# Splitting the first branch's operands during a retention instead of during the rope

## The chip, the cores and the metric

The kernel runs on one core of a Trainium2 chip. The metric is the time of one execution on the device, in microseconds (us). TensorE, the matrix engine, is PE in the profile and its weight loads are PEld; VectorE is DVE, ScalarE is ACT, GpSimd is POOL, and SP is the engine that issues nearly all DMAs.

## What is computed

One block of a hybrid network on 528 tokens (16 meta tokens and 512 of the sequence) with 1024 channels. Cut to what matters here:

```python
z = rms_norm(h) @ w_in
u_rnn, u_gate, q, k, v, g_ret, ga, gb = split(z)
o_a = rg_lru(causal_dwconv(u_rnn)) * gelu(u_gate)
q, k = rotary(q), rotary(k)
o = retention(q, k, v)
o_b = head_rms(o) * silu(g_ret)
mixed = sigmoid(ga) * (o_a @ w_branch_rnn) + sigmoid(gb) * (o_b @ w_branch_ret)
h = h + mixed @ w_out
out = rms_norm(h + conv_ffn(rms_norm(h)))
```

The first branch is `o_a` and its product with `w_branch_rnn`, ten blocks of 128 channels. The retention has four heads.

## The kernel before, in words

Activations stand with channels on the 128 partitions and tokens along the row. TensorE works on fp16 operands: each fp32 operand is split into a high and a low fp16 part, and a product is three matmuls, high by high, high by low and low by high. `split` (L91) makes the two parts: the high one on ACT (L92), a scaled copy, and the low one on DVE (L93), the scaled source minus the high part. Weights come by DMA into two buffers `raw`, are split into ten buffers `wt`, and `tick` moves this on by a step between products.

The stages follow each other in the program: the recurrent branch; its gate; the rope, in which `rotary` (L726) projects q and k of each head in turn (L401) and turns them on DVE (L742 to L744); then scores, values and retention for the heads in the order written at L1014 to L1029; then the branches' products, the output product and the feed-forward part. Up to the rope the order on PE, ACT and DVE is the order of the code. From the rope on, a scheduler sets the order of each engine's instructions when the program is built. Each engine then works in that order.

During the rope of heads 0 and 1, `branch_a` (L713) is called for the ten blocks of the first branch, two or three at a time. It multiplies a block's gate by its recurrent state on DVE (L715; the gate's buffer holds the product) and splits the product into a new buffer `oa`. The parts are first read by `branch` in the stage of gates and branch products, at 426.4 us.

`scores(h)` (L771) makes three groups of products in accumulators `ps`, weighs them on DVE with the decay (`sf`, L794) and splits them (`sc`). `values(h)` makes `v`. `retention_out(h)` (L921) takes four tiles in turn; for each it runs 24 matmuls (L937) and yields after ACT has copied the result to `or` (L941) and squared it (L943) and DVE has added the square to `ssum` (L945). Before the first retention the accumulators are laid out anew, two large ones (`acc`) and four single banks: the new ones lie where the old ones did and wait for these to be read. `gated(0)` follows: `fast_products` (L844) runs gate products in the banks `pa`, `pb` and `pe`, with `kept` and `last` copied out by ACT (L857) and sums on DVE (L874, L878, L885), and `head_norm` (L948) multiplies `ssum` by a matrix of ones on TensorE (L952), takes the root on ACT (L954) and its reciprocal on DVE (L956). Retention of the next head is run between these products.

Of the kernel before, what the change touches and what calls it, by code (L numbers as in the profile page):

```python
# [9 lines left out]
F16 = mybir.dt.float16  # L10
# [4 lines left out]
P = 128  # L15
# [11 lines left out]
TQ = T - T0  # L27
# [9 lines left out]
S_OA = 1.0  # L37
# [14 lines left out]
def hybrid_block_kernel(ctx, tc, x, meta, norm_mix_g, w_in, conv_w, conv_b, rg_a_w, rg_a_b,  # L52
# [12 lines left out]
    def psum_layout(**pools):  # L65

        if "scope" in psum:
            psum["scope"].close()
        psum["scope"] = ExitStack()
        for nm, bufs in pools.items():  # L70
            psum[nm] = psum["scope"].enter_context(tc.tile_pool(
                name="psum_" + nm, bufs=bufs, space=bass.MemoryType.PSUM, reuse_waits="tile"))

    def acc(name):
        return psum["acc"].tile([P, 2, 512], F32, name=name, tag="acc")
# [9 lines left out]
    def piece(shape, dtype, name):  # L85
        return pieces.tile(shape, dtype, name=name, tag="s")

    def wtile(name):
        return work.tile([P, T], F32, name=name, tag="w")

    def split(hi, lo, src, s):  # L91
        a = nc.scalar.activation(hi, src, AF.Copy, scale=s)  # L92
        b = nc.vector.scalar_tensor_tensor(lo, src, s, hi, op0=ALU.mult, op1=ALU.subtract)  # L93
        return a.ins, b.ins
# [193 lines left out]
    def get(u):  # L288
        current[0] = max(current[0], u)
        while len(loaded) <= u:  # L290
            queue(unit_load())
        while done[0] < len(steps) and steps[done[0]][0] <= u:
            emit_step()
        return wviews[u]

    def tick(n=1):

        for _ in range(n):
            if done[0] == len(steps):
                if len(loaded) == len(units):  # L300
                    return
                queue(unit_load())
            u = steps[done[0]][0]
            if sum(unit_tiles(i) for i in range(current[0], u + 1)) > ahead[0]:
                return
            emit_step()
# [401 lines left out]
                for i in range(m0, m0 + 5):  # L708
                    f(i)

    oa = {}

    def branch_a(n):  # L713
        g = gate_g.pop(n)[:, :TQ]
        nc.vector.tensor_mul(g, g, half_x.pop(n)[:, T0:])  # L715
        oa[n] = piece([P, 2, TQ], F16, "oa")
        split(oa[n][:, 0], oa[n][:, 1], g, S_OA)

    order.close()

# [28 lines left out]
    for h in range(HEADS):  # L749
        t = [[piece([P, 2, T], F16, f"qk{h}{i}{m}") for m in range(2)] for i in range(2)]  # L750
        qk.append(t)
        rotary(u_q[h], t[0], HQ, TQ, T0, S_QK / (SW * S_XN))
        if h < 2:
            for n in range(5 * h, 5 * h + 2):
                branch_a(n)
        rotary(u_k[h], t[1], HT, T, 0, S_QK / 16.0 / (SW * S_XN))
        if h < 2:
            for n in range(5 * h + 2, 5 * h + 5):
                branch_a(n)
# [11 lines left out]
    def scores(h):  # L771
        st = sc[h] = [piece([P, 2, n], F16, f"sc{h}") for n in (SOFF[1], SOFF[2] - SOFF[1], SC - SOFF[2])]
        q, k = qk[h]
        krep = work.tile([P, 2, 2, P], F16, name="krep", tag="w")
        for m in range(2):
            nc.vector.tensor_copy(krep[:, m].rearrange("p a (r t) -> p a r t", t=NM),
                                  k[m][:, :, None, T - NM:T].broadcast_to([P, 2, P // NM, NM]))

        def group(pieces):
            ps = acc("ps")  # L780
            for bank, b, c0, n in pieces:
                j0 = JB[b][0]
                i = 0
                for m in range(2):
                    for kk, qq in ((0, 0), (0, 1), (1, 0)):
                        kv = k[m][:, kk, j0:j0 + P] if b < 4 else krep[:, m, kk]
                        nc.tensor.matmul(ps[:, bank, :n], kv,
                                         q[m][:, qq, I0[b] - T0 + c0:I0[b] - T0 + c0 + n],
                                         start=i == 0, stop=i == 5)
                        i += 1  # L790
            for bank, b, c0, n in pieces:
                dc = I0[b] - JB[b][0] + c0
                f = wtile("sf")
                nc.vector.scalar_tensor_tensor(f[:, :n], ps[:, bank, :n], S_S / (S_QK * S_QK),  # L794
                                               dec[h][:, dc:dc + n] if b < 4 else dec_meta[:, h, :n],
                                               op0=ALU.mult, op1=ALU.mult)
                sb = st[SCP[b][0]]
                o = SOFF[b] + c0 - SCP[b][1]
                split(sb[:, 0, o:o + n], sb[:, 1, o:o + n], f[:, :n], 1.0)

        group([(0, 0, 0, 257), (1, 0, 257, 257)])
        group([(0, 1, 0, T - I0[1]), (1, 2, 0, T - I0[2])])
        group([(0, 3, 0, T - I0[3]), (1, 4, 0, T - I0[4])])
# [10 lines left out]
    def make_forms(g):  # L814

        if not x_form_t:
            for i in range(2):
                x_form_t[i] = xslot([P, 4, 4, 257], F16, f"xs{i}")
        ks = slice(2 * g, 2 * g + 2)
        t = {}  # L820
        for i in range(2):
            for j in range(2):
                v = t[i, j] = wtile("xt")[:, :TQ].rearrange("p (k c) -> p k c", k=2)
                k0, (c0, n) = 4 * j + 2 * g, HQ[i]
                nc.vector.tensor_tensor(v, xh[:, k0:k0 + 2, c0:c0 + n], xl[:, k0:k0 + 2, c0:c0 + n], op=ALU.add)
        a11, a12, a21, a22 = t[0, 0], t[0, 1], t[1, 0], t[1, 1]
        nc.vector.tensor_tensor(a22, a22, a21, op=ALU.subtract)
        nc.vector.tensor_tensor(a21, a11, a21, op=ALU.subtract)
        nc.vector.scalar_tensor_tensor(a11, a22, -1.0, a11, op0=ALU.mult, op1=ALU.subtract)
        nc.vector.scalar_tensor_tensor(a12, a11, -1.0, a12, op0=ALU.mult, op1=ALU.subtract)  # L830
        for i, v in enumerate((a12, a22, a11, a21)):
            xs = x_form_t[i // 2]
            split(xs[:, 2 * (i % 2), ks], xs[:, 2 * (i % 2) + 1, ks], v, 1.0)
# [58 lines left out]
    def values(h):  # L892
        vt = []
        wa, wb = get(u_v[h][0]), get(u_v[h][1])
        for b, (j0, nb) in enumerate(JB):
            if b % 2 == 0:
                ps = acc("ps")
            pb = ps[:, b % 2]
            vt.append(piece([P, 2, 512], F16, f"v{h}"))
            i = 0  # L900
            if b == 4:
                for r, wr in enumerate((wa, wb)):
                    for a in range(2):
                        for g in range(4):
                            m = 2 * NM if a == 0 else NM
                            xs = xlast[:, 4 * r + g].rearrange("p a t -> p (a t)")
                            nc.tensor.matmul(pb[32 * g:32 * g + m], xs[:, :m], wr(a, g, 0, 512),
                                             start=r == 0 and a == 0, stop=r == 1 and a == 1,
                                             tile_position=(0, 32 * g))
                split(vt[b][:, 0], vt[b][:, 1], pb, S_V / (SW * S_XN))  # L910
                continue
            for k in range(KD):
                w = wa if k < 4 else wb
                for ax, aw in SPLIT:
                    nc.tensor.matmul(pb, xf(ax, k, XF + j0, nb), w(aw, k % 4, 0, 512), start=i == 0, stop=i == 23)  # L915
                    i += 1
            split(vt[b][:, 0], vt[b][:, 1], pb, S_V / (SW * S_XN))
            tick()
        vv[h] = vt
# [72 lines left out]
    def gated(h):  # L992

        other = retention_out(h + 1)
        for i in range(2):
            a = gate_unit(h, i)
            next(a)
            if i == 0:
                head_norm(h)
            for _ in range(2):  # L1000
                next(a)
                tick()
            next(other)
            scale_head(h, i)
            for _ in range(2):
                next(a)
                tick()
            next(other)
            for _ in a:
                pass  # L1010
        for _ in other:
            pass
# [5 lines left out]
    scores(2)  # L1018
    make_forms(1)
    values(1)  # L1020
    scores(3)
    psum_layout(acc=2, bank=4)
    ahead[0] = 9
    for _ in retention_out(0):
        pass
    gated(0)
    values(2)
    gated(1)
# [601 lines left out]
```

## Time and profile before

| | us |
|---|---|
| median of 3 runs | 1068.04 |
| lowest and highest run | 1067.8, 1068.93 |
| the profiled execution, its own time | 1068.13 |
| its span in the profile | 1066.4 |
| TensorE busy, share of the span | 98% |
| DVE, ACT, POOL | 81%, 55%, 1% |
| mean granted TensorE clock | 0.999 |

The span is what the profiler saw of the execution; the time of a run holds some 1.7 us around it. A busy TensorE is not one at its peak, since matmuls overlap. An engine that is busy all through a stretch does not bind it if TensorE is busy all through it too.

### The profile page before, as it was taken

What the parts mean: (1) busy time and instruction counts of PE and PEld (TensorE: products, weight loads), DVE (VectorE), ACT (ScalarE), POOL (GpSimd) and SP (SyncE); (2) the same over time, 40 slices, a digit from 0 to 9 for tenths busy, and PEclk for the clock granted to TensorE, in tenths of its full rate; (3) what the DMA queues carried; (4) which work ended last, traced back from release to release, by engine and by line L of the source; (5) the groups of instructions that cost most, each with busy time, mean ns of one, the idle gap of its engine ahead of it and who ended that gap; (6) DMA issues with size and microseconds to landing.
All of it is one profiled execution on the core that took longest, in us unless ns stands there. A gap on an engine that the chain in (4) does not pass through costs nothing.

```text
span 1066.4 us, 21008 instructions
## 1 busy us (share of the span) xinstructions
PE 1049.7 (98%) x8995; PEld 851.7 (80%) x8995; DVE 860.2 (81%) x1289; ACT 589.1 (55%) x927; POOL 6.9 (1%) x20
## 2 busy tenths in 40 slices
PE   9999999999999999999999999999999999999997
PEld 6888888865684848888888886588888888888884
DVE  6885799998786969887787886479989897988975
ACT  8568954434564747566454453366566465454442
POOL 2000000000000000000000000000000000000000
PEclk9999999999999999999999999999999999999999
DMA  8331243431211322333333365032432324214322
GB/s 255 102 133 45 80 139 119 160 120 40 78 43 47 113 65 65 115 94 109 115 110 115 105 221 179 1 119 80 159 111 88 120 81 136 64 60 137 102 80 80
DMA packets 108989, 111.49 MB, mean 105 GB/s; under 512 B 5610, under 2 KB 100560, under 8 KB 108896
## 3 DMA queue, kind: packets, MB, share of 16 engines
q1 hardware_dynamic: 108448, 109.74, 32.0%
q8 instruction: 70, 1.15, 0.4%
q10 hardware_dynamic: 160, 0.27, 0.1%
q0 software_dynamic: 288, 0.14, 0.1%
q14 instruction: 23, 0.19, 0.1%
HBM read 108.04 MB, written 2.10 MB: 103 GB/s over the span
## 4 chain that ended last, share of the span: by engine, by line
PE 78%; DVE 14%; ACT 6%; issue 2%; ACTq 0%; DVEq 0%
PE ps L401 31%; PE P L1466 9%; PE pa L852 9%; PE pm L401 4%; PE ps L915 4%; PE ps L1189 4%; PE pe L852 4%; DVE wt L93 3%; PE ps L414 3%; PE pb L852 2%; PE pa L1353 2%; ACT wt L92 2%; PE ps L937 1%; DVE rnn L648 1%; PE pe L1353 1%
## 5 line engine op out<-in xcount | busy, mean ns | idle before, releaser
L401 PEld LDWEIGHTS <-wt 128*128 128x128 f16 x3840 | 373.2, 97 | 58.2 <-DVE t L742 1.4
L93 DVE SCALAR_TENSOR_TENSOR wt<-raw,wt 128x1024 f16<-128x1024 f32 (+2 forms) x278 | 303.9, 1105 | 64.9 <-ACT wt L92 63.6
L92 ACT ACTIVATE wt<-raw 128x1024 f16<-128x1024 f32 (+2 forms) x278 | 263.4, 962 | 151.3 <-PE P L1466 25.3
L852 PEld LDWEIGHTS <-wt 128*128 128x128 f16 x2016 | 195.0, 97 | 34.7 <-issue 7.4
L401 PE MATMUL ps<-x2h,wt 128*128 128x258 f16 x1184 | 181.2, 273 | 0.0
L401 PE MATMUL ps<-xh,wt 128*128 128x257 f16 (+2 forms) x1056 | 163.8, 275 | 1.1 <-DVE t L742 1.1
L401 PE MATMUL ps<-x2l,wt 128*128 128x258 f16 x592 | 113.2, 272 | 0.0
L401 PE MATMUL ps<-xl,wt 128*128 128x257 f16 (+2 forms) x528 | 102.2, 275 | 0.0
L1466 PE MATMUL P<-wt,act 128*128 128x256 f16 x792 | 88.3, 273 | 0.0
L1466 PEld LDWEIGHTS <-act 128*128 128x128 f16 x792 | 77.5, 98 | 9.0
L915 PE MATMUL ps<-wt,xh 128*128 128x512 f16 x256 | 76.1, 379 | 2.3 <-DVE v L93 2.3
L1331 DVE SCALAR_TENSOR_TENSOR cv<-ps,vt,cv 128x512 f32<-128x512 f32 x80 | 59.7, 747 | 22.8 <-ACT cv L1329 21.9
L852 PE MATMUL pa<-xs,wt 128*128 128x257 f16 x576 | 71.6, 273 | 3.4 <-ACT kept L857 3.1
L401 PE MATMUL pm<-oa,wt 128*128 128x257 f16 x480 | 55.4, 274 | 0.0
L1329 ACT ACTIVATE cv<-ps,vt,vt 128x512 f32<-128x512 f32 x40 | 31.0, 774 | 34.5 <-PE ps L401 33.8
L915 PEld LDWEIGHTS <-xh 128*128 128x128 f16 x256 | 24.8, 98 | 31.4 <-issue 3.4
L915 PE MATMUL ps<-wt,xl 128*128 128x512 f16 x128 | 48.3, 379 | 0.0
L256 DVE TENSOR_TENSOR raw<-raw 128x1024 f32<-128x1024 f32 x39 | 47.6, 1220 | 0.7
L852 PE MATMUL pa<-ob,wt 128*128 128x257 f16 x384 | 45.7, 274 | 0.6 <-ACT last L857 0.5
L1189 PE MATMUL ps<-wt,mx 128*128 128x512 f16 x192 | 44.3, 378 | 0.0
L1353 PEld LDWEIGHTS <-wt 128*128 128x128 f16 x336 | 32.6, 97 | 4.4
L1189 PEld LDWEIGHTS <-mx 128*128 128x128 f16 x192 | 17.7, 98 | 18.4
(290 smaller groups left out, 1417.1 us busy)
## 6 DMA issues: line engine op xcount, KB each, us to landing
raw<-in_w_in SPq DMA_DIRECT2D x40, 1024.0 KB, 4.9
raw<-in_w_up SPq DMA_DIRECT2D x24, 1024.0 KB, 5.2
raw<-in_w_down SPq DMA_DIRECT2D x48, 256.0 KB, 3.5
raw<-in_w_branch_ret SPq DMA_DIRECT2D x16, 512.0 KB, 4.5
raw<-in_w_branch_rnn SPq DMA_DIRECT2D x8, 640.0 KB, 4.6
raw<-in_w_out SPq DMA_DIRECT2D x4, 1024.0 KB, 4.9
xin<-in_x SPq DMA_DIRECT2D x4, 512.0 KB, 5.5
raw<-in_w_in SPq DMA_DIRECT2D x4, 512.0 KB, 8.1
```

The lines of the kernel that those rows point to most:

```text
L92: a = nc.scalar.activation(hi, src, AF.Copy, scale=s)
L93: b = nc.vector.scalar_tensor_tensor(lo, src, s, hi, op0=ALU.mult, op1=ALU.subtract)
L256: nc.vector.tensor_tensor(pair, pair, rv[:, :, right].rearrange("p (h k) c -> p h k c", h=2), op=ALU.add)
L401: nc.tensor.matmul(ps[:, hf, :n], w(aw, k, col, P), src(ax, k, c0, n), start=k == 0 and (aw, ax) == (0, 0), stop=k == nk - 1 and aw == 1)
L414: mm = nc.tensor.matmul(ps[:, hf, :n], w(aw, k, col, P), src(ax, k, c0, n), start=k == 0 and (aw, ax) == (0, 0), stop=k == KD - 1 and aw == 1)
L852: nc.tensor.matmul(ps[:, :257], ws[k // 4](wf, aw, k % 4), src(xf_, ax, k), start=first and k == 0 and (aw, ax) == (0, 0), stop=k == last_ ...
L915: nc.tensor.matmul(pb, xf(ax, k, XF + j0, nb), w(aw, k % 4, 0, 512), start=i == 0, stop=i == 23)
L1189: nc.tensor.matmul(ps[:, n], mx[k][:, a, c0:c0 + P], wo[k // 2](aw, k % 2, n * 512, 512), start=k == 0 and (a, aw) == (0, 0), stop=k == ks ...
L1329: nc.scalar.activation(vv_, src[:, :, 2:258], AF.Identity, scale=vt2[:, 96 + ch:97 + ch], bias=bias)
L1331: nc.vector.scalar_tensor_tensor(vv_, src[:, :, j:j + 256], vt2[:, 48 * j + ch:48 * j + ch + 1], vv_, op0=ALU.mult, op1=ALU.add)
L1353: nc.tensor.matmul(ps[:, :258], w(wf, aw, k), x2_form(xf_, ax, k), start=first and k == 0 and (aw, ax) == (0, 0), stop=k == 3 and aw == 1, ...
L1466: nc.tensor.matmul(pd[:, 256 * tt:256 * tt + 256], t[:, ax, c0 + tt * P:c0 + tt * P + P], w(wf, aw, i), start=q % 6 == 0 and tt == 0 and i ...
```

## The change

`branch_a` keeps the product and no longer splits it. A new `split_a` splits the next two products that are not split yet. It is called once after `values(1)` and, in place of `pass`, after each of the four tiles of the first retention, for all ten.

```diff
-    oa = {}
+    oa, products_a = {}, []
 
     def branch_a(n):
         g = gate_g.pop(n)[:, :TQ]
         nc.vector.tensor_mul(g, g, half_x.pop(n)[:, T0:])
-        oa[n] = piece([P, 2, TQ], F16, "oa")
-        split(oa[n][:, 0], oa[n][:, 1], g, S_OA)
+        products_a.append(g)
+
+    def split_a(m=2):
+        for _ in range(m):
+            n = len(oa)
+            oa[n] = piece([P, 2, TQ], F16, "oa")
+            split(oa[n][:, 0], oa[n][:, 1], products_a[n], S_OA)
...
     values(1)
+    split_a()
     scores(3)
     psum_layout(acc=2, bank=4)
     ahead[0] = 9
     for _ in retention_out(0):
-        pass
+        split_a()
     gated(0)
```

Lines behind `branch_a` stand five further down in the changed kernel, those behind the call after `values(1)` six. Three places of the order show it. The first is DVE in the rope of head 0, from the last split of its q to the splits of its k; `oa<-rnn` are the splits, `rnn<-rnn` the multiplications, `t` the rope's products. Before:

```order
L93 SCALAR_TENSOR_TENSOR oa<-rnn,oa 128x514 x2
L742 TENSOR_TENSOR t_2092<-ps,rope_1850 128x528
L715 TENSOR_TENSOR rnn<-rnn 128x514
L93 SCALAR_TENSOR_TENSOR wt<-raw,wt 128x1024 x2
L715 TENSOR_TENSOR rnn<-rnn 128x514
L743 TENSOR_TENSOR t_2093<-ps,rope_1851 128x528
L742 TENSOR_TENSOR t_2097<-ps,rope_1850 128x528
```

and changed:

```order
L747 TENSOR_TENSOR t_2086<-ps,rope_1850 128x528
L715 TENSOR_TENSOR rnn<-rnn 128x514
L93 SCALAR_TENSOR_TENSOR wt<-raw,wt 128x1024 x2
L715 TENSOR_TENSOR rnn<-rnn 128x514 x3
L748 TENSOR_TENSOR t_2087<-ps,rope_1851 128x528
L747 TENSOR_TENSOR t_2091<-ps,rope_1850 128x528
```

Two splits have gone and two multiplications, which stood further back, have come ahead of the last two products. The second place is DVE at the end of `values(1)`, where the scores of head 3 begin. Before:

```order
L93 SCALAR_TENSOR_TENSOR v_3372<-ps,v_3372 128x512
L93 SCALAR_TENSOR_TENSOR v_3403<-ps,v_3403 128x512
L794 SCALAR_TENSOR_TENSOR sf<-ps,dec_2873 128x257 x2
L794 SCALAR_TENSOR_TENSOR sf<-ps,dec_2873 128x400
L93 SCALAR_TENSOR_TENSOR sc_3422<-sf,sc_3422 128x257 x2
```

and changed:

```order
L93 SCALAR_TENSOR_TENSOR v_3342<-ps,v_3342 128x512
L93 SCALAR_TENSOR_TENSOR v_3373<-ps,v_3373 128x512
L93 SCALAR_TENSOR_TENSOR oa<-rnn,oa 128x514 x2
L799 SCALAR_TENSOR_TENSOR sf<-ps,dec_2843 128x257 x2
L799 SCALAR_TENSOR_TENSOR sf<-ps,dec_2843 128x400
L93 SCALAR_TENSOR_TENSOR sc_3398<-sf,sc_3398 128x257 x2
```

Two splits stand ahead of the `sf` products. The third place is ACT in the first retention, from the first tile's copy to the first `kept`. Before:

```order
L941 ACTIVATE or_3498<-ps 128x514
L943 ACTIVATE ssum<-ps 128x514
L941 ACTIVATE or_3499<-ps 128x514
L943 ACTIVATE sq<-ps 128x514
L941 ACTIVATE or_3500<-ps 128x514
L943 ACTIVATE sq<-ps 128x514
L941 ACTIVATE or_3501<-ps 128x514
L943 ACTIVATE sq<-ps 128x514
L857 ACTIVATE kept<-pa 128x257
```

and changed:

```order
L946 ACTIVATE or_3474<-ps 128x514
L948 ACTIVATE ssum<-ps 128x514
L92 ACTIVATE oa<-rnn 128x514 x2
L946 ACTIVATE or_3475<-ps 128x514
L948 ACTIVATE sq<-ps 128x514
L92 ACTIVATE oa<-rnn 128x514 x2
L946 ACTIVATE or_3476<-ps 128x514
L948 ACTIVATE sq<-ps 128x514
L92 ACTIVATE oa<-rnn 128x514 x2
L946 ACTIVATE or_3477<-ps 128x514
L948 ACTIVATE sq<-ps 128x514
L92 ACTIVATE oa<-rnn 128x514 x2
```

A pair of splits stands behind each tile's square, the last one ahead of `kept`. On TensorE one matmul of the product `pe` stands ahead of the ones matmuls of `head_norm` that stood behind them; nothing else moves there.

## Rows read from the trace of the kernel before

**Rows 1.** The page, part 1: busy time, share of the span, instructions.

```profile
PE 1049.7 (98%) x8995; PEld 851.7 (80%) x8995; DVE 860.2 (81%) x1289; ACT 589.1 (55%) x927; POOL 6.9 (1%) x20
```

**Rows 2.** Windows: length, busy time per engine (instructions), granted clock, DMA share, GB/s.

```profile
161.70:226.70 65.00, 65.00 (x578) 56.13 (x579) 63.41 (x88) 27.62 (x39) 0.00 (x0) 1.00 0.47 156
226.70:285.70 59.00, 58.35 (x369) 30.55 (x367) 50.91 (x101) 26.93 (x49) 0.00 (x0) 1.00 0.11 39
380.00:385.00 5.00, 3.55 (x17) 1.55 (x16) 3.49 (x6) 0.93 (x2) 0.00 (x0) 1.00 0.00 0
```

**Rows 3.** The chain of waits, 130 to 330 us: start, length, what.

```profile
161.70 65.04 PE ps L401 x576
...
293.43 0.60 ACT or L941
...
295.39 1.11 PE ps L952 x4
```

**Rows 4.** Order of time in the rope: start, length, instruction, [idle before <-releaser].

```profile
161.70 0.40 PE L401 MATMUL ps<-xh,wt 128*128 128x257 f16 x2 [1.12 <-DVE t L742]
...
164.02 1.14 ACT L92 ACTIVATE oa<-rnn 128x514 f16<-128x514 f32 x2
...
165.10 1.29 DVE L93 SCALAR_TENSOR_TENSOR oa<-rnn,oa 128x514 f16<-128x514 f32 x2
...
171.02 0.70 DVE L742 TENSOR_TENSOR t<-ps,rope 128x528 f32<-128x528 f32 x1
...
172.60 0.39 PE L401 MATMUL ps<-xl,wt 128*128 128x264 f16 x2
...
224.08 0.63 ACT L92 ACTIVATE wt<-raw 128x512 f16<-128x512 f32 x1 [1.95 <-PE ps L401]
...
224.74 0.69 DVE L93 SCALAR_TENSOR_TENSOR wt<-raw,wt 128x512 f16<-128x512 f32 x1 [1.26 <-ACT wt L92]
```

**Rows 5.** The tile `oa`: count, ns min/median/max, first and last start.

```profile
L92 ACT ACTIVATE oa<-rnn x10: 616/616/618, 164.0 to 198.4; 128x514 f16<-128x514 f32 x10
L93 DVE SCALAR_TENSOR_TENSOR oa<-rnn,oa x10: 684/685/686, 165.1 to 200.3; 128x514 f16<-128x514 f32 x10
```

**Rows 6.** DVE in order of time, from the last values split to the gate.

```profile
283.67 1.28 DVE L93 SCALAR_TENSOR_TENSOR v<-ps,v 128x512 f16<-128x512 f32 x2
284.87 0.75 DVE L794 SCALAR_TENSOR_TENSOR sf<-ps,dec 128x257 f32<-128x257 f32 x2
...
287.19 0.65 DVE L794 SCALAR_TENSOR_TENSOR sf<-ps,dec 128x272 f32<-128x272 f32 x2
...
294.55 0.69 DVE L945 TENSOR_TENSOR ssum<-ssum,sq 128x514 f32<-128x514 f32 x1 [1.16 <-ACT sq L943]
...
297.34 3.36 DVE L956 RECIPROCAL rt<-rt 128x514 f32<-128x514 f32 x1
...
303.68 0.43 DVE L878 TENSOR_TENSOR g<-pe,last 128x257 f32<-128x257 f32 x1
```

**Rows 7.** ACT in order of time, the first retention.

```profile
288.31 0.58 ACT L941 ACTIVATE or<-ps 128x514 f32<-128x514 f32 x1
288.79 0.59 ACT L943 ACTIVATE ssum<-ps 128x514 f32<-128x514 f32 x1
...
293.93 0.59 ACT L943 ACTIVATE sq<-ps 128x514 f32<-128x514 f32 x1
294.83 0.39 ACT L857 ACTIVATE kept<-pa 128x257 f32<-128x257 f32 x1 [0.31 <-PE pa L852]
```

**Rows 8.** PE in order of time, from the first retention to the gate.

```profile
285.72 7.67 PE L937 MATMUL ps<-sc,v 128*128 128x257 f16 x96
293.25 0.27 PE L852 MATMUL pa<-xh,wt 128*128 128x257 f16 x1
...
297.22 1.49 PE L852 MATMUL pa<-xs,wt 128*128 128x257 f16 x12
...
306.25 0.27 PE L852 MATMUL pe<-xh,wt 128*128 128x257 f16 x1
```

## The prediction, made before the result was known

> **What bounds the kernel now.** I read the page first: TensorE is busy for 1049.7 us of a span of 1066.4 [rows 1]. Nearly all of the time is matmuls, so an edit can only add to or take from the 16.7 us in which TensorE is idle. Then I read the windows of the two stretches that the change touches. Through the rope and after it (161.70 to 226.70) TensorE is busy 65.00 of 65.00 us although DVE is too (63.41); through scores and values (226.70 to 285.70) it idles 59.00 - 58.35 = 0.65 us; its 1.12 us of idle before 161.70 is the only other one near [rows 2, 4]. The chain of waits says the same: one unbroken piece of 65.04 us on TensorE in the rope, and in the first head's retention a hand-over from the last `or` on ACT to the ones matmul of `head_norm` (L952) [rows 3]. So the rope is bound by TensorE with a busy DVE beside it, and the retention is where ACT and DVE end a wait.
>
> **What the rope gives back.** Ten splits leave it. Two of them in a row take 1.14 us on ACT and 1.29 us on DVE [rows 4]; with one alone at 616 ns and 685 ns [rows 5], the second starts 0.52 us after the first on ACT and 0.605 us on DVE. So ACT loses 5.2 us and DVE 6.05 us of work there. I cost this at nothing, for three reasons. The one wait of TensorE (1.12 us, ended at 161.70 by the rope's first product, L742) comes before the first `oa` split on DVE, at 165.10, and what stands ahead of that product is unchanged. From then on TensorE waits for nobody. And the lead that DVE gains is lost before it could matter: at 224.74 DVE stands idle for a weight split by ACT, and ACT's at 224.08 had itself waited for TensorE to free a buffer [rows 4]. From there the scores run as before, with their 0.65 us of idle.
>
> Could the new order cost something in the rope? The next key projection starts at 172.60, and its accumulator is freed by the L742 product that starts at 171.02 and ends at 171.72 [rows 4]: 0.88 us of slack. Ahead of that product two splits (1.21 us) go and two more multiplications L715 come. Their price is that of the L742 product (0.70 us long, about 0.6 us from start to start): 1.2 us, so the slack stays. ACT does two weight splits ahead of one `qk` split, which the scores read 50 us later. SP keeps its order of loads, and its buffers come free earlier, if at all; POOL has no part in it. The products now wait in their fp32 buffers in place of the `oa` pieces, so the count of buffers held is the same until the splits run.
>
> **The first pair, after values(1).** On DVE it stands between the last values split and the first `sf` product of head 3's scores. The two values splits begin at 283.67 and the `sf` at 284.87; two splits more make that 284.87 + 2 x 0.605 = 286.08 [rows 6]. Their high halves on ACT have nothing of the scores ahead of them and are ready in time. Who waits: head 0's first retention tile takes an accumulator that the first group of scores held, and this is free when the second `sf` is through, at 284.87 + 0.75 = 285.62; TensorE enters at 285.72 [rows 6, 8]. There is 0.10 us between, so no slack: TensorE comes in 1.21 us late, at 286.93. The second tile waits for the `sf` at 287.19 [rows 6], which moves by the same 1.21 us. **+1.21 us.**
>
> **The four pairs in the retention.** ACT evacuates a tile with `or` (288.31) and a square (288.79), 0.48 us each from start to start [rows 7]; a pair adds 2 x 0.52 = 1.04 us. A round on ACT is then 2.00 us, one on TensorE 7.53 / 4 = 1.88 us (96 matmuls from 285.72 to the next product at 293.25) [rows 8]. There are two accumulators, so ACT sets the pace. Its queue, moved by the 1.21 us of the scores: `or` at 289.52, then every 2.00 us: 291.52, 293.52, 295.52; the last square at 296.00 where it was at 293.93 [rows 7], which is 2.07 us later. TensorE loses 0.1 us on the fourth tile (the second square ends at 292.6, its third tile at 292.6), then runs the twelve matmuls of `pa` and five of `pe`, and stands before the ones matmul. That follows the last sum of squares, DVE at 294.55 before, TensorE at 295.39 [rows 3, 6], so it moves by the 2.07 us to 297.46. TensorE's queue now has one matmul of `pe` ahead of it that stood behind: 0.11 us back. **+0.75 us more, together +1.96, say +2.0 us.**
>
> Two readings of a pair's price differ. The trace has the second of two splits start before the first has ended, 1.14 us against 2 x 0.616 [rows 4, 5]. [...]
>
> **What stays hidden.** Behind the last square stand ACT's last pair and then `kept`, which moves from 294.83 to about 297.5 and ends at 297.9; TensorE needs it for the product at 297.22 + 1.96 = 299.2 [rows 7, 8]. On DVE the reciprocal (297.34, 3.36 us long) waits behind a weight split whose ACT half stands right behind `kept`, so it moves by the 2.7 us of `kept`. The sum L878 that followed at 303.68 [rows 6] comes at 306.4 at the latest and ends at 306.8; TensorE reads it for the product at 306.25 + 1.96 = 308.2 [rows 8]. That is 1.4 us of slack, so nothing. From here everything follows TensorE, with the same waits as before, later.
>
> **Sum.** Profiled execution 1068.13 us, span 1066.40; plus 2.0 gives 1070.1 us. The median of the runs, 1068.04, is 0.09 below that execution. What could be unknown is the overlap of the pairs with the work around them. From below: they fit into ACT's pauses and only the first pair costs, +1.2. From above: TensorE overlaps with none of the eight halves, 1.21 + 8 x 0.52 = +5.4. I take the rows' own distances, since they are rows of these very splits. A gain cannot be more than the idle time in the two stretches, 1.12 + 0.65 = 1.8 us.
>
> **Rivals.**
> - *Slower, clearly.* Between `or` and a square, each split takes its full length. Then six splits between the first `or` and the last square cost 6 x 0.096 = 0.58 us more on ACT, the first pair 2 x 0.08 = 0.16 us on DVE: +2.7, 1070.9 us. It is decided by whether a split starts before its neighbour's end. For it: each pair stands beside readers of PSUM, which the row of two splits does not show. Against: `or` to square are 0.48 us apart and overlap [rows 7].
> - *Hidden.* ACT's round hides behind TensorE's and only the entry costs: 1068.13 + 1.2 = 1069.3 us. For it: before, ACT's 0.96 us of work per tile left it 0.9 us free. Against: a pair needs 1.04 us. [...]
> - *The rope pays.* A lighter DVE removes the 1.12 and the 0.65 us: 1070.1 - 1.8 = 1068.3 us. Against: both idles stand where DVE's queue is unchanged or already waits for TensorE [rows 2, 4].
> - *It does not move.* Excluded: the order shows the splits at their new places and no other work of TensorE displaced.
>
> [...]
>
> **How the numbers follow.** A measurement of this kernel tells about 0.2% from no change, 2.1 us. The forecast (+2.0, give or take 0.3) has 0.62, of which 0.42 lies within that bound and 0.20 above it; clearly slower 0.18; hidden 0.15; the rope pays 0.03; 0.02 is left for a gain in a place that I have not seen. Slower is 0.20 + 0.18 = 0.38, the same 0.42 + 0.15 + 0.03 = 0.60, faster 0.02. The range runs from just above the rope's case, 1068.4, past the hidden and the clearly slower one with the forecast's own give, 1071.2.
>
> **What would show it.** Right: TensorE unbroken through the rope and DVE idle there for some 6 us; `sf` near 286.1 and the first retention tile near 286.9; `or` 2.0 us apart; the ones matmul near 297.5 with about 1 us of idle before it; every later stage about 2 us late. Wrong: a first tile at 285.7, `or` 1.9 us or less apart, a TensorE wait in the rope, or a later stage that takes the 2 us back.

## The result, and the profile after

| | before | changed |
|---|---|---|
| median of 20 runs, us | 1067.86 | 1070.08 |
| lowest and highest run, us | 1067.71, 1069.43 | 1069.73, 1072.33 |
| the profiled execution, own time, us | 1068.13 | 1070.65 |
| its span, us | 1066.4 | 1068.9 |
| mean granted TensorE clock | 0.999 | 0.999 |

The ratio of the two is 1.0021, with an interval from 1.0014 to 1.0027: 2.2 us slower, where +2.0 us (1070.1) was forecast.

Before two executions are laid beside each other, their starts have to be compared. The profiled execution of the changed kernel is 0.25 us ahead from the start on: a marker of the first stage, the `pmeta` matmul of L519, stands at 12.46 us before and at 12.21 us after. Behind it nothing differs up to the rope. So 0.25 us is added to every start below before it is set against a row of before.

The page, part 1, of the changed kernel:

```profile
PE 1049.5 (98%) x8995; PEld 851.6 (80%) x8995; DVE 860.6 (81%) x1289; ACT 588.5 (55%) x927; POOL 6.9 (1%) x20
```

No engine's busy time tells the two kernels apart [rows 1]: the work is the same. The windows, with the columns of [rows 2]: the rope, scores and values, and the first retention.

```profile
161.70:226.70 65.00, 65.00 (x580) 56.14 (x578) 57.79 (x79) 22.98 (x29) 0.00 (x0) 1.00 0.49 163
226.70:285.70 59.00, 58.25 (x366) 30.41 (x365) 50.97 (x100) 27.45 (x49) 0.00 (x0) 1.00 0.09 32
285.70:300.00 14.30, 12.41 (x134) 10.85 (x134) 13.29 (x27) 11.89 (x25) 0.00 (x0) 1.00 0.28 97
```

In the rope DVE has lost 5.6 us of work (63.41 to 57.79) and ACT 4.6 us, and TensorE is busy 65.00 of 65.00 us as it was: nothing is won there. The first retention shows where the time goes: TensorE is idle for 14.30 - 12.41 = 1.89 us. The waits of TensorE between 150 and 330 us (who waits and for whom; us in total, times, the longest) split this up:

```profile
PE ps L401 <- DVE t L747: 1.1, 1, 1.1
PE ps L942 <- DVE sf L799: 1.0, 1, 1.0
PE ps L957 <- DVE ssum L950: 1.0, 1, 1.0
```

The first of the three was there before [rows 4]. The second is new, and the third was 0.2 us. TensorE in order of time:

```profile
286.62 7.78 PE L942 MATMUL ps<-sc,v 128*128 128x257 f16 x96 [1.01 <-DVE sf L799]
294.26 0.27 PE L857 MATMUL pa<-xh,wt 128*128 128x257 f16 x1
...
295.58 0.72 PE L857 MATMUL pe<-xs,wt 128*128 128x257 f16 x5
297.26 1.11 PE L957 MATMUL ps<-ssum,ones 128*128 128x257 f32 x4 [0.96 <-DVE ssum L950]
298.20 0.94 PE L857 MATMUL pe<-xs,wt 128*128 128x257 f16 x7
```

The entry stood at 285.72 [rows 8] and is at 286.62 + 0.25 = 286.87, 1.15 us later. From the entry to the `pa` product behind the ones matmul (298.98 here, a row of the same view) it took 297.22 - 285.72 = 11.50 us before and takes 298.98 - 286.62 = 12.36 us now, 0.86 us more. Together 2.01 us. Of the 0.86 us, 0.74 are the longer wait before the ones matmul (0.96 against 0.22 us), and 0.11 us are lost in the tiles (7.78 against 7.67 us [rows 8]). At the entry the recorded idle time, 1.01 us, is smaller than the delay of 1.15 us: it is counted from the end of the last matmul's record, and the records overlap (one matmul of `pa` or `pe` is recorded as 0.27 us long, five in a row take 0.72 us). So delays are read from starts here, not from idle times. ACT in the retention shows the round:

```profile
289.27 0.58 ACT L946 ACTIVATE or<-ps 128x514 f32<-128x514 f32 x1
289.75 0.59 ACT L948 ACTIVATE ssum<-ps 128x514 f32<-128x514 f32 x1
290.23 1.15 ACT L92 ACTIVATE oa<-rnn 128x514 f16<-128x514 f32 x2
291.27 0.59 ACT L946 ACTIVATE or<-ps 128x514 f32<-128x514 f32 x1
...
293.27 0.61 ACT L946 ACTIVATE or<-ps 128x514 f32<-128x514 f32 x1
...
295.27 0.63 ACT L946 ACTIVATE or<-ps 128x514 f32<-128x514 f32 x1
295.75 0.64 ACT L948 ACTIVATE sq<-ps 128x514 f32<-128x514 f32 x1
```

No row carries an idle time any more, and `or` comes every 2.00 us: ACT's queue sets the pace. Before, the last square stood at 293.93 [rows 7]. On DVE the pair stands ahead of `sf`, as the order had it:

```profile
284.62 1.28 DVE L93 SCALAR_TENSOR_TENSOR oa<-rnn,oa 128x514 f16<-128x514 f32 x2
285.82 1.23 DVE L799 SCALAR_TENSOR_TENSOR sf<-ps,dec 128x257 f32<-128x257 f32 x3
...
296.42 0.69 DVE L950 TENSOR_TENSOR ssum<-ssum,sq 128x514 f32<-128x514 f32 x1
```

One more thing happened in this execution: at 643 us TensorE waited 0.7 us for a `kept`, which it did not do in the kernel before. In ACT's queue this `kept` stands behind two splits of the output weights, and ACT waited 5.13 us for their load, against 3.42 us before. The profile of the changed kernel is thus 2.5 us longer and not 2.0. Whether that belongs to the change is one of the questions below.

### The profile page after: what moved, and what is told of

Read it like the earlier page. It is cut to its first block, busy times and chain, and to the rows that moved or that the text cites. A ratio compares the mean times of both kernels' runs of the same rounds, so it can differ in the third digit from the quotient of the medians.

```text
span 1068.9 us, 21006 instructions
## 1 busy us (share of the span) xinstructions
PE 1049.5 (98%) x8995; PEld 851.6 (80%) x8995; DVE 860.6 (81%) x1289; ACT 588.5 (55%) x927; POOL 6.9 (1%) x20
## 3 DMA queue, kind: packets, MB, share of 16 engines
q8 instruction: 70, 1.15, 0.5%
## 4 chain that ended last, share of the span: by engine, by line
PE 71%; DVE 16%; ACT 9%; issue 2%; DMA 1%; ACTq 0%; DVEq 0%
PE ps L401 29%; PE P L1472 9%; PE pa L857 7%; PE pm L401 4%; DVE wt L93 4%; PE ps L920 4%; PE ps L1195 4%; PE ps L414 3%; PE pe L857 3%; ACT wt L92 2%; PE pa L1359 2%; PE pb L857 2%; DVE rnn L648 1%; DVE raw L256 1%; PE pe L1359 1%
## 5 line engine op out<-in xcount | busy, mean ns | idle before, releaser
L942 PE MATMUL ps<-sc,v 128*128 128x257 f16 (+4 forms) x384 | 32.3, 236 | 1.0 <-DVE sf L799 1.0
```

The lines of the kernel that those rows point to most:

```text
L942: nc.tensor.matmul(ps[:, hf, s0 - lo_i:257], vt[b][:, va, d * P:(d + 1) * P], st[SCP[b][0]][:, sa, o:o + hi_i - s0], start=i == 0, stop=i ...
```

## The experiments

Theory: what the change costs is one wait at the entry (the first pair, on DVE, ahead of `sf`) and one round of ACT that is longer than TensorE's (the four pairs); the rope gives nothing back. The rivals: ACT's queue alone; the splits cost wherever they stand; the rope pays. Differences are medians of 9 to 11 runs against 12 to 33 of the kernel before on the same chip; an interval is about 1 us to either side, so between neighbours in the table the trace decides.

| run | where the ten splits stand | ratio, interval | difference, us |
|---|---|---|---|
| c1 | as changed | 1.0019, 1.0011 to 1.0028 | +2.00 |
| e1 | 2 rope, 2 behind each tile | 1.0012, 1.0003 to 1.0021 | +1.23 |
| e2 | 2 behind values(1), 8 rope | 1.0013, 1.0005 to 1.0022 | +1.19 |
| e3 | 2 behind scores(3), 2 behind each tile | 1.0018, 1.0009 to 1.0027 | +1.86 |
| e4 | 6 in values(2), 4 in values(3) | 0.9998, 0.9989 to 1.0007 | -0.12 |
| f1 | 1 behind each tile, 6 in values(2) | 1.0002, 0.9994 to 1.0011 | +0.04 |
| f2 | 2 behind each tile, 2 in values(2) | 1.0007, 0.9998 to 1.0016 | +0.80 |
| f3 | 3, 3, 3, 1 behind the tiles | 1.0009, 1.0001 to 1.0018 | +0.98 |
| h1 | as changed; ones matmuls later | 1.0004, 0.9995 to 1.0013 | +0.30 |
| g3 | as e4; multiplications held back | 0.9988, 0.9980 to 0.9997 | -1.21 |
| g4 | as before; multiplications held back | 1.0001, 0.9992 to 1.0010 | +0.03 |
| b1 | as g3; ones matmuls later | 0.9976, 0.9966 to 0.9986 | -2.56 |

**c1, the changed kernel once more.**

> The changed kernel once more, beside the experiments. Its first profile was 2.5 us longer than the one of the kernel before, of which 2.0 us arose in the first retention and before it, and some 0.7 us between 634 and 647 us, at a load of the output weights. My theory: that 0.7 us belongs to that one execution; the wait of 0.7 us there is absent, and the time is +2.0 us, near 1069.9. Rival: the changed order brings the wait along, then it is there again and the time is +2.5 us.

It came out at +2.00 us. In its profile the wait at the late load is gone; of the waits for `kept`, 3.8 us in six in the first profile, 3.1 us in five are left, which is what the kernel before has:

```profile
PE pa L857 <- ACT kept L862: 3.1, 5, 1.1
```

Between 640 and 650 us TensorE's one wait is 0.5 us, for a `last`, in c1 and in the kernel before alike. So the 0.7 us is put down to the slower load of that one execution, and the change itself costs 2.0 us.

**e2, the entry alone.** Against the changed kernel:

```diff
     values(1)
-    split_a()
+    split_a(0, 1)
     scores(3)
...
     for _ in retention_out(0):
-        split_a()
+        pass
```

with `split_a` taking the numbers of the blocks, and the other eight split in `branch_a`.

> Only the first pair stands behind values(1); the other eight splits are in the rope as before. My theory: the entry wait of 1.0 us before the first retention tile stays, the retention behind it runs as in the kernel before (`or` at TensorE's pace of about 1.88 us, ones matmul without a new wait), so +1.2 us against the kernel before, near 1069.1. Rival 'the pairs in the retention make all of it' gives 0.0, 1067.9; rival 'a wait at the entry is taken back later by slack' also 0.0, but with the 1.0 us wait in the trace.

Measured +1.19 us. TensorE in order of time:

```profile
286.62 7.72 PE L943 MATMUL ps<-sc,v 128*128 128x257 f16 x96 [1.02 <-DVE sf L800]
...
296.35 1.11 PE L958 MATMUL ps<-ssum,ones 128*128 128x257 f32 x4 [0.21 <-DVE ssum L951]
```

The entry waits as in the changed kernel, the ones matmul as in the kernel before. The entry alone is worth its 1.2 us, and nothing later takes it back.

**e1, the four pairs with the first pair left in the rope.**

```diff
     def branch_a(n):
...
         products_a.append(g)
+        if n < 2:
+            split_a(1)
...
     values(1)
-    split_a()
     scores(3)
```

> The first pair of splits is back in the rope, the other four stay in the retention. My theory (the cost is an entry wait of 1.21 us from the pair behind values(1), and 0.75 us from ACT's round of 2.00 us): the entry wait before the first retention tile falls from 1.0 us to 0.2 us or less, `or` stays 2.00 us apart but its first one starts about 288.3, the ones matmul waits about 1 us and starts about 296.2; the execution is +0.75 us against the kernel before, near 1068.6 to 1068.7. Rival 'ACT's queue alone sets the end of the retention, wherever the entry is' would keep +2.0 us. Rival 'the entry alone costs' gives +0.0 us, 1067.9.

Measured +1.23 us, half a microsecond above what I had worked out. The retention was as expected: from the entry to the `pa` product behind the ones matmul it took 298.47 - 286.16 = 12.31 us, 0.81 us more than before. The rest was a place that I had not looked at, in the rope:

```profile
178.24 1.90 DVE L715 TENSOR_TENSOR rnn<-rnn 128x514 f32<-128x514 f32 x3
180.06 2.35 DVE L93 SCALAR_TENSOR_TENSOR wt<-raw,wt 128x1024 f16<-128x1024 f32 x2
182.33 0.69 DVE L750 TENSOR_TENSOR t<-ps,rope 128x514 f32<-128x514 f32 x1
182.93 0.68 DVE L749 TENSOR_TENSOR t<-ps,rope 128x514 f32<-128x514 f32 x1
```

In the kernel before, three `oa` splits (1.8 us) stood ahead of these turning products, the second of which began at 182.43. In their place the scheduler put two more weight splits (2.3 us), so the products came 0.5 us later, and TensorE, which waits for the second of them, resumed late:

```profile
183.76 0.38 PE L401 MATMUL ps<-xh,wt 128*128 128x257 f16 x2 [0.22 <-DVE t L749]
```

In the kernel before, this projection begins at 183.32; with the 0.05 us between the two starts that is 0.39 us earlier than here. The retention's 0.81 us and these 0.39 us make 1.20 us.

**f2, the four pairs without that.** `split_a()` behind each tile, none at the entry, the last two in values(2), none in the rope.

> A pair behind each of the four tiles as in the changed kernel, the other two splits in values(2), none in the rope and none at the entry. It is the run of the four pairs alone, without the wait of 0.4 us that the pair left in the rope brought. My theory: `or` 2.00 us apart from 288.3 on, ones matmul with a wait of about 1 us, +0.8 us against the kernel before, near 1068.9. Rival 'the pairs cost 1.2 us wherever the first one stands': +1.2 us, 1069.3.

Measured +0.80 us, with `or` at 288.27, 290.28, 292.28, 294.28 and the ones matmul waiting 0.96 us. The pairs cost 0.8 us, the entry 1.2 us, and the two add up to c1.

**e3, the pair behind the scores.** Only its call moves:

```diff
     values(1)
-    split_a()
     scores(3)
+    split_a()
     psum_layout(acc=2, bank=4)
     ahead[0] = 9
```

> The first pair's call stands behind scores(3), so that on DVE it comes after the last products of the scores, and ahead of the first retention tile's `or` on ACT. My theory: the entry wait of 1.0 us goes (first tile near its place in the kernel before), but ACT's queue in the retention begins about 1 us later (two splits, 1.04 us, ahead of the first `or`), so that the last square and the ones matmul come about 1.8 us later than in the kernel before: +1.8 us, near 1069.7, hardly another time than the changed kernel, with the wait moved from the entry to the tiles and the ones matmul. Rival 'the entry wait is a cost by itself': +0.75 us, 1068.6.

Measured +1.86 us. The wait changed its place and hardly its size:

```profile
285.56 3.97 PE L942 MATMUL ps<-sc,v 128*128 128x257 f16 x48
290.32 4.02 PE L942 MATMUL ps<-sc,v 128*128 128x257 f16 x48 [0.79 <-ACT ssum L948]
...
297.19 1.11 PE L957 MATMUL ps<-ssum,ones 128*128 128x257 f32 x4 [0.96 <-DVE ssum L950]
```

The first tile starts at its old place; the third waits for an accumulator, because on ACT the pair now stands ahead of the first `or`. With the entry wait away and the same halves still ahead in ACT's queue, +1.86 us stood against +2.00: less than the interval tells apart.

**f1, one split behind each tile.** The other six splits stand in values(2).

```diff
     values(1)
-    split_a()
     scores(3)
...
-    for _ in retention_out(0):
-        split_a()
+    first = retention_out(0)
+    for m in (1, 1, 1, 1):
+        next(first)
+        split_a(m)
+    for _ in first:
+        pass
```

> No split in the rope or at the entry; one behind each of the four tiles of the first retention, the other six in values(2). My theory (a split costs TensorE time only while it makes ACT's round longer than TensorE's): ACT's round is 0.96 + 0.52 = 1.48 us against TensorE's 1.88 us, so `or` stays about 1.86 us apart, the ones matmul waits 0.2 us as in the kernel before, and the time is +0.0 us, near 1068. Rival 'each split near the readers of PSUM costs its 0.52 us or a part of it': four halves, +0.4 to +2.1 us.

Measured +0.04 us. ACT in the middle of the retention:

```profile
290.90 0.65 ACT L92 ACTIVATE oa<-rnn 128x514 f16<-128x514 f32 x1
291.72 0.60 ACT L948 ACTIVATE or<-ps 128x514 f32<-128x514 f32 x1 [0.17 <-PE ps L944]
```

There is idle time before `or` again, and it waits for TensorE: one split fits into ACT's round (1.48 us of work, beside 1.88 us on TensorE), two, with 2.00 us, do not.

**f3, three behind a tile.** The same edit with (3, 3, 3, 1), and none in values(2).

> All ten splits in the retention, three behind each of the first three tiles and one behind the last. My theory: ACT's round is 0.96 + 3 x 0.52 = 2.52 us; `or` at about 288.3, 290.8, 293.4, 295.9, last square 2.4 us later than in the kernel before, ones matmul +2.4, less 0.1 for the `pe` matmul: +2.3 us, near 1070.4. Rival 'a fixed cost of a busy ACT in the retention, not one by the split': +0.8 us as with pairs, 1068.9. Rival 'DVE's three splits a round, 1.8 us and 0.6 us of sum, set the pace': the round would be 2.4 us on DVE, below ACT's, so no more than +2.3 us.

Measured +0.98 us, not +2.3. ACT did what was expected: `or` stands at 288.08, 290.61, 293.13 and 295.65, 2.52 us apart. What was not expected is on TensorE:

```profile
291.74 2.00 PE L942 MATMUL ps<-sc,v 128*128 128x257 f16 x24 [0.44 <-ACT sq L948]
...
294.92 1.50 PE L857 MATMUL pe<-xs,wt 128*128 128x257 f16 x12
...
297.64 1.11 PE L957 MATMUL ps<-ssum,ones 128*128 128x257 f32 x4 [0.56 <-DVE ssum L950]
```

The ones matmul is indeed 2.5 us later than before (297.64 + 0.25 against 295.39), but all twelve `pe` matmuls and six of the next product `pb` now stand ahead of it, where four of `pe` did. The scheduler's order has filled the time. What was lost is little more than the idle time, 0.44 + 0.56 us against 0.22 before. So this late result was not priced by its lateness, 2.5 us, but by what TensorE had left to do: +0.98 us. In the changed kernel the scheduler moved one matmul only.

**h1, the ones matmuls behind the product.** In the changed kernel, `head_norm` is called one step later, in every head:

```diff
-            if i == 0:
-                head_norm(h)
-            for _ in range(2):
+            for j in range(2):
                 next(a)
                 tick()
+                if i == 0 and j == 0:
+                    head_norm(h)
```

> The changed kernel, with the ones matmuls of head_norm behind all twelve matmuls of the `pe` product: seven of them, 0.11 us each, stand ahead that stood behind. ACT's round stays as it is. My theory (a late sum of squares costs only what TensorE has no other work for): the ones matmul starts no earlier, near 297.3, but its wait falls from 1.0 us to about 0.2 us, so -0.77 us against the changed kernel: +1.2 us against the kernel before, near 1069.1. Rival 'the root and the reciprocal behind it are the path': no gain, +2.0 us.

Measured +0.30 us, that is 1.70 us below c1. The expected part is there, with ACT's round unchanged:

```profile
295.67 1.50 PE L857 MATMUL pe<-xs,wt 128*128 128x257 f16 x12
297.36 1.11 PE L957 MATMUL ps<-ssum,ones 128*128 128x257 f32 x4 [0.19 <-DVE ssum L950]
```

0.77 us of the wait are gone. The other 0.9 us come from the later heads, where the call moves too: the first read of `oa` on TensorE stands at 426.7 us here and at 428.7 in c1, and with starts 0.4 us apart that is 1.6 us won by then. TensorE's waits of the whole span show a shorter one for `v` (2.3 us in c1) and a longer one for `kept`:

```profile
PE pa L857 <- ACT kept L862: 3.6, 6, 1.1
...
PE ps L920 <- DVE v L93: 1.2, 3, 0.5
```

What in the later heads did this was not tried apart.

**e4, the splits in values(2) and values(3).**

```diff
             split(vt[b][:, 0], vt[b][:, 1], pb, S_V / (SW * S_XN))
+            if b == 0 and h > 1:
+                split_a(6 if h == 2 else 4)
             tick()
```

and none elsewhere.

> All ten splits are taken out of the rope and out of the retention, and stand in values(2) (six) and values(3) (four), where ACT and DVE have some 6 us of idle time. It tells what their removal from the rope is worth by itself. My theory: nothing, so 0.0 us against the kernel before, 1067.9 (+-0.3), with DVE idle some 6 us in the rope and TensorE unbroken there. Rival 'the rope pays': up to -1.8 us, 1066.1. Rival 'splits cost wherever they stand': +1 to +2 us.

Measured -0.12 us. ACT runs six in a row where it stood idle, and the next `v` still waits for TensorE (3.77 us, where it waited 6.90 us before):

```profile
329.60 3.23 ACT L92 ACTIVATE oa<-rnn 128x514 f16<-128x514 f32 x6
336.60 0.60 ACT L92 ACTIVATE v<-ps 128x512 f16<-128x512 f32 x1 [3.77 <-PE ps L920]
```

The rope by itself pays nothing, and the ten splits cost nothing in values(2) and values(3): before this `v` ACT had 6.90 us, of which six of them take 3.13.

**g3, the multiplications held back.** Can the time that DVE gains in the rope be spent? Four of the multiplications L715 stand ahead of the wait of 1.1 us that ends at 161.70; the scheduler had put them early, between the scans of the recurrent branch. On top of e4:

```diff
     def branch_a(n):
         g = gate_g.pop(n)[:, :TQ]
-        nc.vector.tensor_mul(g, g, half_x.pop(n)[:, T0:])
+        with tc.issue_after(turn_last[0].ins):
+            nc.vector.tensor_mul(g, g, half_x.pop(n)[:, T0:])
...
-            nc.vector.tensor_mul(v2_, pp[1 - m][:, :, :nh], sn)
+            turn_last[0] = nc.vector.tensor_mul(v2_, pp[1 - m][:, :, :nh], sn)
```

> The kernel with all ten splits in values(2) and values(3), and besides the multiplications of the first branch are issued behind the last turning product of the head's q or k at hand, so that four of them (0.6 us each on DVE, 2.4 us) no longer stand ahead of the rope's first products. It asks whether DVE time that the moved splits freed in the rope can be used for the 1.1 us wait of TensorE that ends at 161.7. My theory: one weight split (1.14 us) comes forward in their place, DVE still reaches the turning product about 1.2 us earlier, the wait goes and the time is -1.1 us, near 1067.0. Rival 'the load of weights sets DVE's pace there': 0.0 us. Rival 'four weight splits in a row ahead of the next turning products make TensorE wait later': 0.0 to +1 us.

Measured -1.21 us, faster than the kernel before. DVE in order of time, and the window ahead of 161.70:

```profile
159.42 0.68 DVE L748 TENSOR_TENSOR t<-ps,rope 128x514 f32<-128x514 f32 x1
...
164.86 4.61 DVE L93 SCALAR_TENSOR_TENSOR wt<-raw,wt 128x1024 f16<-128x1024 f32 x4
169.40 0.69 DVE L749 TENSOR_TENSOR t<-ps,rope 128x528 f32<-128x528 f32 x1
170.01 0.69 DVE L748 TENSOR_TENSOR t<-ps,rope 128x528 f32<-128x528 f32 x1
```

```profile
150.00:161.70 11.70, 11.70 (x104) 9.81 (x102) 11.70 (x15) 4.64 (x5) 0.00 (x0) 1.00 0.45 144
```

TensorE is busy all through the 11.70 us. The turning product that it had waited for stands at 159.42; before, it stood at 160.95 (this execution starts 0.4 us earlier).

**g4, the same hold with the splits in the rope.**

> The kernel before with only its multiplications held back behind the turning products; the ten splits stay in the rope. It asks whether the gain of 1.2 us, seen with the splits away, needs the splits away. My theory: the wait of 1.1 us at the rope's first product goes, but DVE in the rope of head 0 then has two splits and four weight splits ahead of the next key projection's turning products, which end near 171.9 where TensorE wants them at about 171.5: some 0.4 us is given back there, -0.7 us in all, near 1067.2. Rival 'the splits' place has no part in it': -1.2 us. Rival 'DVE is full in the rope (63.4 of 65.0 us busy) and all is given back': 0.0 us.

Measured +0.03 us: the rival was right, all of it is given back. The wait has gone from 161.7 to the next key projection:

```profile
164.37 0.68 DVE L93 SCALAR_TENSOR_TENSOR oa<-rnn,oa 128x514 f16<-128x514 f32 x1
...
165.59 0.68 DVE L93 SCALAR_TENSOR_TENSOR oa<-rnn,oa 128x514 f16<-128x514 f32 x1
166.19 4.62 DVE L93 SCALAR_TENSOR_TENSOR wt<-raw,wt 128x1024 f16<-128x1024 f32 x4
...
171.35 0.69 DVE L743 TENSOR_TENSOR t<-ps,rope 128x528 f32<-128x528 f32 x1
```

```profile
172.19 0.39 PE L401 MATMUL ps<-xh,wt 128*128 128x264 f16 x2 [1.07 <-DVE t L743]
```

I had reckoned with 0.4 us there. The two `oa` splits at 164.37 and 165.59 make the turning products 1.3 us later than in g3 (171.35 against 170.01, with starts 0.1 us apart), and TensorE, ahead by 1.1 us, stands for 1.07 us. So the hold pays only with the splits out of the rope, and moving them out pays only with the hold.

**b1, the three edits that won, together.**

> Three edits together: the ten splits in values(2) and values(3), the multiplications held back behind the turning products, and head_norm's ones matmuls behind the `pe` product in every head. My theory: the edits act in different places and add. The first two gave -1.2 us; the third gave -1.7 us against the changed kernel, of which 0.8 us was the wait that the pairs had made and that is only 0.2 us here, and the rest came in the later heads (the wait for `v` 1.1 us shorter, the one for `kept` 0.5 us longer). So -1.2 - 0.2 - 0.9 = -2.3 us against the kernel before, near 1065.6. Rival 'the splits in values(2) and values(3) take the place that the later heads' gain needs': -1.4 us, 1066.5.

Measured -2.56 us, against -2.3 worked out: the fastest kernel of the study. Of TensorE's waits the two at the rope and at the sum of squares are gone, and the one for `v` is 1.1 us:

```profile
PE pa L858 <- ACT kept L863: 3.6, 6, 1.1
PE ps L481 <- DVE warm L476: 1.5, 1, 1.5
PE ps L921 <- DVE v L93: 1.1, 3, 0.5
```

## Why the prediction was right

*What the rope gives back.* Priced at nothing. TensorE is unbroken there, DVE stands idle for 6.7 us in five waits (2.81, 2.69, 0.56, 0.37 and 0.31 us), and e4 takes all ten splits out of the rope at -0.12 us. The reason held too: the one wait ahead of the rope hangs on DVE's queue before the first split. What the prediction did not see is that this queue held four multiplications that could be held back; g3 shows that the rival "the rope pays" is right for another kernel, and wrong for this change alone. The step "the slack of 0.88 us stays" held for the changed kernel, but the slack was read too large: the row at 172.60 holds the third and fourth matmul of the key projection, its first two start at 172.38, and so the slack was 0.66 us. With other orders the rope did give way, in g4 at this same place and in e1 at a later one.

*The first pair.* +1.21 us predicted; 1.15 us at the entry, +1.19 us in e2.

*The four pairs.* +0.75 us predicted from a round of 2.00 against 1.88 us; 2.00 us in the trace, 0.86 us in the changed kernel, 0.80 us in f2. The ones matmul was to start near 297.5 and starts at 297.26 + 0.25 = 297.51, after 0.96 us of idle where about 1 was said. f1 and f2 stand on either side of TensorE's round: 1.48 and 2.00 us against 1.88.

*What stays hidden.* The last pair, `kept` and the reciprocal (which begins at 299.82) bring no new wait of TensorE up to 330 us.

*The sum.* +2.0 us; +2.22 us in the first comparison, +2.00 us in c1. The terms miss by -0.06 and +0.11 us and their sum by 0.05 us. The two misses belong together: the ones matmul follows ACT's queue, whose last square stands at 295.75 + 0.25 = 296.00, just where the prediction had it, so what TensorE did not lose at the entry it waited longer there.

*"Slower, clearly"* was the rival with splits at full length. The trace refutes it in a telling way: the ACT halves did become longer.

```profile
L92 ACT ACTIVATE oa<-rnn x10: 625/644/677, 283.4 to 296.7; 128x514 f16<-128x514 f32 x10
```

616 ns is now 644 ns in the middle and up to 677 ns [rows 5]. And still the next `or` starts 1.04 us after a pair begins (290.23 to 291.27). In the rope, too, a split was 616 ns long and the next one started 0.52 us after it. The start-to-start distance, not the length, belonged in the sum over this queue.

*"Hidden"* fell because ACT's round is the longer one with a pair, and f1 (+0.04 us) shows that it would have held with a single split: there all of the evacuation is hidden (1.48 us of ACT work beside 1.88 us of matmuls). In f2 (+0.80 us) the two overlap as well, but a round of 2.00 us does not fit into 1.88.

*The clock* stayed at its full level: 1.00 was granted in all three windows, among them the one with the two waits and 1.89 us of idle time, as in the window with 1.45 us of it in the kernel before (380 to 385) [rows 2].

## What to carry to other kernels

Where two engines hand tiles to each other, compare their rounds in start-to-start distances. Here the shorter round, 0.96 us on ACT, left 0.9 us a tile beside TensorE's 1.88: one split more, 0.52 us, cost 0.04 us in all (f1), and two, 1.04 us, cost 0.80 us (f2). Time freed on a full but hidden engine was worth nothing here until the work that stands ahead of the bound engine's wait was moved into it; the two edits paid together (g3, -1.21 us) and neither alone (e4, -0.12, and g4, +0.03 us). And a result that came 2.5 us late cost 0.98 us (f3), since TensorE had other matmuls queued for most of that time, so look at what stands behind the waiting instruction before cutting the work that makes it late.

## What the runs showed that was not expected

In the changed kernel's unbroken ACT queue the instructions are recorded as longer without taking more of the queue's time: `or` goes from 0.58 to 0.63 us along the four tiles, and an `oa`, 616 ns long in the kernel before, takes up to 677 ns, while `or` keeps coming every 2.00 us.

Profiled executions of one and the same stage differ by up to 0.6 us at their start (the `pmeta` marker at 12.04 us in g3, 12.46 in the kernel before, 12.66 in c1), and one showed a wait of 0.7 us at a load that a second one did not. Effects below a microsecond were to be read only from distances inside a stage.
